# Transposing x on TensorE, pacing the modulation by matmuls issued, and loading early weights from GpSimd's queue

## The chip, the cores and the metric

One core of a Trainium2 chip runs the program. The metric is device time in microseconds of one execution; before the change its median is 1635.82 us over three runs. The engines are TensorE (PE, matmuls; PEld is its weight load), VectorE (DVE), ScalarE (ACT), GpSimd (POOL) and SyncE (SP, which here only issues DMAs). Each engine works through its own instructions in order.

## What is computed

A residual block on x of 512 x 2048: adaLN modulation, one wide projection, two branches (dilated attention and mLSTM), two output projections and a last norm. The early stage, which the change touches, is this part of the reference:

```python
mod = c @ w_ada[l] + b_ada[l]
shift, scale, gate = jnp.split(mod, 3, axis=-1)
h = rmsnorm(x, norm_gain[l]) * (1.0 + scale[:, None]) + shift[:, None]
proj = h @ w_in[l]
```

All is float32. Each product of float32 matrices is made of three matmuls on rounded parts: `a = hi + lo`, and hi\*hi, hi\*lo and lo\*hi are summed.

## The kernel before

h is held transposed: 16 tiles, k = 0 to 15, each of 128 features by 512 positions. The early stage makes these tiles one by one and multiplies each at once.

For one k these steps are needed, with their names in the code. (a) Modulation: four passes of DVE (L338, `modulation`), two halves of 1024 for scale and two for shift, each over a 512 KB tile `y` of `ada`, 64 in all. Call one pass a half. (b) A small product `gs` on DVE (L393), then ACT applies scale and shift to x (L396, `modulated`) and casts it to its rounded part, the tile `ha` or `hb` (L172, in `split`); the rest of that split, `lo`, is a subtraction (L173), which GpSimd makes for k > 0. (c) The stationary weights come as `ws[k]`, 128x768, in two parts of 384: ACT casts each to `hi`, DVE subtracts to `lo`. Then 18 matmuls of 512 columns (`first_products`, L280) add to six PSUM banks.

Ten more column blocks of the projection, the extras (`extra_products`), are not accumulated over all k in PSUM. They are done in five groups of k (`GROUPS`), so (g, n) is 6 matmuls for the short groups 0 and 4, and 12 for the long ones. The table `TURNS` tells after which k each pair of extras is issued. For group 0 ACT copies the PSUM bank to SBUF (L515), for later groups DVE adds it to what is there (L517). Their weights' `lo` parts are made by GpSimd. In all the stage has 288 matmuls of first products and 480 of extras.

Order: nothing is scheduled by a tool. Each engine's order is the order of the code. `prepare` issues the casts and subtractions of weights about three parts ahead of their matmuls, `hi` and `lo` have four buffers each, and `modulate(n)` issues halves until n are done. Before the change it is called so that the four halves of the next k are spread over the matmuls of this k (`next_pieces`). SP issues all loads from one list, `loads`: `y`, and weights into `raw` (three buffers) and `more` (one). x comes already transposed (`xT`), four of the 16 tiles ahead of the constants.

The norm's statistic (`first_norm`): ACT squares the 16 tiles, PE and DVE sum them over features, and the reciprocal root stands as 128x512, one value for each position in each partition. Each tile is multiplied by it (L388, `normed`), the first on DVE and the others on GpSimd, four k ahead.

After this stage come the V projection of the mLSTM (`vblock`, matmuls of 258 columns), and then all the rest of the program.

Of the kernel before, what the change touches and what calls it, by code (L numbers as in the profile page):

```python
# [104 lines left out]
def block_kernel(ctx: ExitStack, tc, xT, x, c, cst, abias, ada, ws, wu, wv, fgain, out):  # L105
# [72 lines left out]
    stream, loads, pieces, ready, late, tasks, beside = [], [], [], [], [], [], []  # L178
    at = {"load": 0, "split": 0, "half": 0, "piece": 0, "raw": 0, "more": 0, "y": 0}
# [9 lines left out]
    def add(u):  # L189
        stream.append(u)  # L190
        loads.append(u)

    def load_ahead():
        while at["load"] < len(loads):
            u = loads[at["load"]]
            if u.ring == "any":
                u.ring = "raw" if at["raw"] < RAW or "more" not in tags else "more"
            if at[u.ring] == {"raw": RAW, "more": MORE, "y": ADA}[u.ring]:
                if u.ring == "more":
                    u.ring = "any"  # L200
                break
            if u.at_load:
                u.at_load()
            u.raw = S(u.ring)
# [4 lines left out]
    def prepare():
# [9 lines left out]
        else:  # L219
# [75 lines left out]
    def load_x(n):  # L295
        for _ in range(n):
            t = S("gm")
            dma(t, xT[len(xt)])
            xt.append(t)
# [1228 lines left out]
```

## Time and profile before

| | us |
|---|---|
| median of three runs (1635.78 to 1636.86) | 1635.82 |
| the profiled execution | 1637.23 |
| its span, first to last instruction | 1635.4 |
| first matmul of the early stage's products starts | 36.07 |
| last one starts, and the V projection's first | 246.54, 246.77 |

The profile shows, for each engine, when an instruction ran and what ended the wait ahead of it. The granted clock is given as a share of 2.4 GHz, so 0.50 is the lower level of 1.2 GHz. A matmul's duration holds the pipeline's drain, so for matmuls in a row the distance between starts is what counts.

### The profile page before, as it was taken

The page shows a single profiled execution, that of the slowest core. Times are in us where ns is not written, and L with a number is a line of the kernel's source. Part 1 is how long each engine was busy: PE and PEld are TensorE (multiplying, and loading weights), DVE is VectorE, ACT ScalarE, POOL GpSimd, SP SyncE. Part 2 cuts the span into 40 slices and gives each one's busy share as a digit, 9 for nine tenths or more (in the row PEclk, how much of TensorE's full clock was granted, in tenths as well). Part 3 has the DMA queues.
Part 4 walks back from the last instruction along what each step waited for, and adds up shares of the span by engine and source line. Part 5 has one row for each costly group of instructions (what it writes and reads, how often), then busy time and mean ns, then how long its engine had stood idle before and what let it go on. Part 6 is the DMA issues. An engine that isn't in the chain of part 4 may idle for free.

```text
span 1635.4 us, 24961 instructions
## 1 busy us (share of the span) xinstructions
PE 1565.2 (96%) x9686; PEld 1388.3 (85%) x9686; DVE 1147.9 (70%) x1933; ACT 704.6 (43%) x1189; POOL 139.8 (9%) x112
## 2 busy tenths in 40 slices
PE   3799899999999999999999999999999999999997
PEld 1576689988888888999999999999999788878887
DVE  6788867667746568888788887888896444474445
ACT  3332344335525434455454454454443843343234
POOL 2665540000000000000000000000000000000000
PEclk7999999999999999999999999999999999999999
DMA  8677735665222344344443444444444654432333
GB/s 313 241 276 273 272 113 168 223 217 179 90 94 74 104 163 159 139 152 130 142 144 124 146 145 137 144 142 132 133 161 149 216 176 137 176 105 95 125 117 129
DMA packets 93879, 260.01 MB, mean 159 GB/s; under 512 B 10424, under 2 KB 14648, under 8 KB 93760
## 3 DMA queue, kind: packets, MB, share of 16 engines
q1 hardware_dynamic: 79928, 233.24, 41.6%
q10 hardware_dynamic: 13832, 25.18, 4.4%
q8 instruction: 76, 1.25, 0.3%
q14 instruction: 43, 0.35, 0.1%
HBM read 229.02 MB, written 29.36 MB: 158 GB/s over the span
## 4 chain that ended last, share of the span: by engine, by line
PE 71%; DVE 13%; issue 6%; ACT 4%; DMA 3%; POOL 1%; SPq 0%; ACTq 0%; DVEq 0%; POOLq 0%
PE ps L280 47%; PE ps L807 23%; DVE y L338 3%; DVE lo L173 2%; ACT sh L172 2%; DVE cs L780 1%; DVE e L822 1%; DVE cs L784 1%; DVE cs L785 1%; DMA raw<-ws 1%; DVE sl L173 1%; DVE al L786 1%; DMA p<-kept 1%; DMA more<-ws 1%; ACT gm L396 1%
## 5 line engine op out<-in xcount | busy, mean ns | idle before, releaser
L173 DVE TENSOR_TENSOR lo<-raw,hi 128x512 fp32r<-128x512 f32 (+2 forms) x238 | 177.5, 751 | 172.1 <-ACT hi L172 171.7
L172 ACT CAST hi<-raw 128x512 fp32r<-128x512 f32 (+3 forms) x276 | 161.2, 596 | 277.9 <-PE ps L280 227.4
L807 PE MATMUL ps<-t,sh 128*128 128x256 f32 x1344 | 245.3, 282 | 0.0
L807 PEld LDWEIGHTS ps<-t,sh 128*128 128x128 f32 x1344 | 208.0, 190 | 0.0
L807 PE MATMUL ps<-t,sl 128*128 128x256 f32 x672 | 189.3, 282 | 0.0
L779 ACT CAST ah<-raw 128x768 fp32r<-128x768 f32 x112 | 93.6, 836 | 204.8 <-issue 105.2
L280 PE MATMUL ps<-ha,hi 128*128 128x512 f32 x384 | 126.5, 409 | 26.1 <-ACT ha L172 17.2
L173 DVE TENSOR_TENSOR sl<-cs,sh 128x1024 fp32r<-128x1024 f32 x112 | 137.3, 1226 | 16.0 <-ACT sh L172 15.7
L172 ACT CAST sh<-cs 128x1024 fp32r<-128x1024 f32 x112 | 117.6, 1050 | 67.8 <-DVE cs L785 67.4
L786 DVE TENSOR_TENSOR al<-raw,ah 128x768 fp32r<-128x768 f32 x112 | 106.9, 955 | 52.8 <-ACT ah L779 52.6
L280 PE MATMUL ps<-hi,h 128*128 128x512 f32 (+1 forms) x512 | 143.6, 366 | 0.0
L280 PE MATMUL ps<-hi,ha 128*128 128x258 f32 (+1 forms) x512 | 129.8, 339 | 0.0
L280 PE MATMUL ps<-hi,hb 128*128 128x258 f32 (+1 forms) x512 | 129.3, 339 | 0.0
L807 PEld LDWEIGHTS ps<-t,sl 128*128 128x128 f32 x672 | 127.8, 190 | 0.0
L280 PE MATMUL ps<-hb,hi 128*128 128x512 f32 x384 | 122.0, 397 | 1.6 <-POOL hb L173 1.6
L280 PEld LDWEIGHTS ps<-ha,hi 128*128 128x128 f32 x384 | 73.9, 195 | 48.3 <-ACT ha L172 19.2
L280 PEld LDWEIGHTS ps<-hi,h 128*128 128x128 f32 x512 | 91.8, 188 | 17.0
L807 PE MATMUL ps<-hb,ah 128*128 128x256 f32 x448 | 87.1, 287 | 11.5 <-DVE e L822 9.9
L280 PEld LDWEIGHTS ps<-hi,ha 128*128 128x128 f32 x512 | 87.8, 188 | 11.4 <-issue 0.4
L280 PEld LDWEIGHTS ps<-hi,hb 128*128 128x128 f32 x512 | 87.9, 188 | 10.8
L280 PE MATMUL ps<-lo,h 128*128 128x512 f32 (+1 forms) x256 | 93.9, 367 | 2.4 <-DVE lo L173 2.4
L280 PE MATMUL ps<-h,hi 128*128 128x512 f32 x286 | 89.6, 395 | 0.0
(276 smaller groups left out, 3461.8 us busy)
## 6 DMA issues: line engine op xcount, KB each, us to landing
raw<-wu SPq DMA_DIRECT2D x223, 512.0 KB, 3.6
y<-ada SPq DMA_DIRECT2D x64, 512.0 KB, 7.3
g<-kept SPq DMA_DIRECT2D x56, 256.0 KB, 3.9
kept<-e ACTq DMA_DIRECT2D x56, 256.0 KB, 2.5
raw<-ada SPq DMA_DIRECT2D x24, 512.0 KB, 3.7
more<-wu SPq DMA_DIRECT2D x16, 512.0 KB, 3.5
raw<-wv SPq DMA_DIRECT2D x12, 516.0 KB, 3.7
kept<-g ACTq DMA_DIRECT2D x20, 256.0 KB, 4.2
```

Of the source, the lines that this page charges most:

```text
L172: nc.scalar.copy(hi, src)
L173: (low or nc.vector).tensor_tensor(lo, src, as32(hi), ALU.subtract)
L280: nc.tensor.matmul(ps, a, b, start=first and n == 0, stop=last and n == 2)
L338: nc.vector.tensor_tensor_reduce(out=raw[:, :1024], in0=raw[:, :1024], in1=cb[half][:, :1024], scale=1.0, scalar=bmod[:, col : col + 1] if ...
L396: nc.scalar.activation(xt[k], xt[k], AF.Identity, bias=mods[:, k : k + 1], scale=gs)
L779: nc.scalar.copy(ah, r[:, HT : 4 * HT])
L780: nc.vector.tensor_tensor(two(s[:, : 2 * HT]), two(r[:, HT : 3 * HT]), r[:, :HT].unsqueeze(1).to_broadcast([P, 2, HT]), ALU.add,)
L784: nc.vector.tensor_tensor(s[:, 2 * HT : 3 * HT], s[:, :HT], r[:, 2 * HT : 3 * HT], ALU.add)
L785: nc.vector.tensor_tensor(s[:, 3 * HT :], s[:, 2 * HT : 3 * HT], r[:, 3 * HT : 4 * HT], ALU.add)
L786: nc.vector.tensor_tensor(al, r[:, HT : 4 * HT], as32(ah), ALU.subtract)
L807: nc.tensor.matmul(banks[bank][:, n * HT : (n + 1) * HT], x[:, w], y, start=count[bank] == 1, stop=count[bank] == 24 * len(BANKS[bank]),)
L822: nc.vector.tensor_tensor(v[:, 0:2, :], twice(v[:, 4, :]), two(bb), ALU.add)
```

## The change

- x is loaded as it lies, 16 tiles of 128 positions by 512 features, tile j\*4+t. The squares are summed along the rows as they are made (ten on ACT, six on DVE), so the statistic is one column for each of four tiles. `normed(j)` scales the four tiles of 512 features (for j = 0 two on ACT and two on DVE, for j = 1 to 3 all on ACT), and `turned(k)` transposes on PE: four 128x128 transposes into one PSUM bank, which ACT copies to SBUF (for k = 0 modulation reads the bank itself). `turned(0..3)` stand ahead of the first products, then two after each of the first products k = 0 to 5; `normed(1)` stands in `first_norm`, `normed(2)` and `normed(3)` after the first products of k = 1 and k = 3.
- All subtractions that GpSimd made, of h and of the extras' weights, are made on DVE.
- `TURNS`: all ten extras of group 0 are issued after k = 1; none after k = 2, 3 and 4. From k = 5 the table is as before.
- Pacing: the number of halves issued follows the number of matmuls issued, 6 plus one for each ten, with the need of the next k as a floor.
- Loads: `loads` is two lists. `y` stays on SP's queue; weights into `raw` and `more` are issued from GpSimd's queue as long as the pool `heads` is open (through the V_A blocks), and need not stand behind `y`.

Line numbers of the kernel after are about 2 to 26 higher. The core of the diff:

```diff
 TURNS = {
-    1: [(0, 0)], 2: [(0, 2), (0, 4)], 3: [(0, 6)], 4: [(0, 8)],
+    1: [(0, 0), (0, 2), (0, 4), (0, 6), (0, 8)],
     5: [(1, 0), (1, 2)], 6: [(1, 4)], 7: [(1, 6)], 8: [(1, 8)],
...
-            dma(u.raw[:, : u.width], u.src)
...
+                (nc.gpsimd if "heads" in open_parts and u.ring != "y" else nc.sync).dma_start(u.raw[:, : u.width], u.src)
...
     def first_norm():
...
+        for j in range(NT):
+            for t in range(NT):
+                to, junk = sums[:, t, j : j + 1], S("hb")
+                if (j * NT + t) % 8 in (2, 5, 7):
+                    nc.vector.tensor_tensor_reduce(
...
+                else:
+                    nc.scalar.activation(junk, xn[j][t], AF.Square, accum_out=to)
...
+        nc.vector.tensor_reduce(rstd, sums, mybir.AxisListType.X, ALU.add)
+        nc.scalar.activation(rstd, rstd, AF.Sqrt, bias=eps, scale=1.0 / D)
         nc.vector.reciprocal(rstd, rstd)
-        rs.append(rstd)
-        normed(0, nc.vector)
+        normed(0, True)
+        for k in range(4):
+            turned(k)
         modulate(3)
         for _ in range(2):
             prepare()
         modulate(4)
-        for k in range(1, 4):
-            normed(k, nc.gpsimd)
+        normed(1)
...
+    def normed(j, both=False):
+
+        for t in range(NT):
+            r = rstd[:, t : t + 1]
+            if both and t % 2:
+                nc.vector.tensor_scalar(xn[j][t], xn[j][t], r, None, ALU.mult)
+            else:
+                nc.scalar.activation(xn[j][t], xn[j][t], AF.Copy, scale=r)
+
+    def turned(k):
+
+        ps = PS("m")
+        for t in range(NT):
+            nc.tensor.transpose(ps[:, t * P : (t + 1) * P], xn[k // 4][t][:, k % 4 * P : (k % 4 + 1) * P], ident)
+        if k == 0:
+            xt.append(ps)
+        else:
+            xt.append(S("hb" if k < HK else "gm"))
+            nc.scalar.copy(xt[k], ps)
...
-            split(xt[k], a, b, nc.gpsimd if k else None)
+            split(xt[k], a, b)
...
+    AHEAD, PACE = 2, 10
+    emitted = [0]
+
+    def next_pieces(n):
+
+        emitted[0] += n
+        modulate(4 + AHEAD + emitted[0] // PACE)
...
+            if half == 1 and k < 6:
+                for i in range(2 * k + 4, 2 * k + 6):
+                    turned(i)
+                if k % 2 == 1 and k < 4:
+                    normed(k // 2 + 2)
...
-                Unit(next(src)[:, :width], width, [extra_products(g, n), extra_products(g, n + 1)], low=nc.gpsimd)
...
+                Unit(next(src)[:, :width], width, [extra_products(g, n), extra_products(g, n + 1)])
```

How the order moves, at three places. On ACT, between the modulated tiles of k = 3 and k = 4, before (gm_101 is x of k = 4, raw_345 holds the weights of k = 3, more_391 those of two extras):

```order
L172 CAST hi_469<-raw_345 128x384
L515 COPY g_474<-ps_460 128x512
L172 CAST hi_485<-raw_345 128x384
L515 COPY g_489<-ps_476 128x512
L172 CAST hi_509<-more_391 128x256
L515 COPY g_513<-ps_491 128x512
L172 CAST hi_526<-more_391 128x256
L396 ACTIVATE gm_101<-gm_101,mods,gs_542 128x512
```

The same place after (hb_325 is x of k = 4, gm_661 and gm_668 those of k = 10 and 11, gm_117 to gm_123 the four tiles of `normed(3)`, raw_531 holds the weights of k = 5):

```order
L172 CAST hi_643<-raw_499 128x384
L409 COPY gm_661<-ps_656 128x512
L409 COPY gm_668<-ps_663 128x512
L398 ACTIVATE gm_117<-gm_117,rstd 128x512
L398 ACTIVATE gm_119<-gm_119,rstd 128x512
L398 ACTIVATE gm_121<-gm_121,rstd 128x512
L398 ACTIVATE gm_123<-gm_123,rstd 128x512
L172 CAST hi_680<-raw_531 128x384
L420 ACTIVATE hb_325<-hb_325,mods,gs_685 128x512
```

The copies of the extras are gone from here, and two copies of transposes and four scalings stand ahead of the cast hi_680.

On DVE, up to the last half for k = 6 and its `gs`, before:

```order
L173 TENSOR_TENSOR lo_644<-raw_498,hi_643 128x384
L338 ISA y_614,mods<-y_614,w_134,acc_641 128x1024
L338 ISA mods 128x1
L338 ISA y_616,acc_697<-y_616,w_133,bmod 128x1024
L338 ISA acc_697 128x1
L338 ISA y_618,mods<-y_618,w_134,acc_697 128x1024
L338 ISA mods 128x1
L393 TENSOR_TENSOR gs_717<-mods,cs 128x1
```

And after (ps_846 and ps_864 are the banks of the last two extras that are issued ahead of k = 6; ha_892 is its rounded tile):

```order
L542 TENSOR_TENSOR g_451<-g_451,ps_846 128x512
L340 ISA y_678,acc_879<-y_678,w_132,bmod 128x1024
L340 ISA acc_879 128x1
L173 TENSOR_TENSOR lo_884<-raw_738,hi_883 128x512
L542 TENSOR_TENSOR g_477<-g_477,ps_864 128x512
L340 ISA y_693,mods<-y_693,w_133,acc_879 128x1024
L340 ISA mods 128x1
L414 TENSOR_TENSOR gs_889<-mods,cs 128x1
L173 TENSOR_TENSOR ha_892<-hb_389,ha_892 128x512
```

The last half of k = 6 now stands behind the sum that reads the last extra's bank, and the subtraction for h has come to DVE, right behind `gs`.

On GpSimd, behind the broadcasts of c, before:

```order
L388 TENSOR_TENSOR gm_94<-gm_94,w_164 128x512
L388 TENSOR_TENSOR gm_96<-gm_96,w_164 128x512
L388 TENSOR_TENSOR gm_98<-gm_98,w_164 128x512
L388 TENSOR_TENSOR gm_101<-gm_101,w_164 128x512
L173 TENSOR_TENSOR ha_293<-gm_94,ha_293 128x512
L388 TENSOR_TENSOR gm_103<-gm_103,w_164 128x512
L173 TENSOR_TENSOR lo_318<-raw_159,hi_317 128x256
```

And after:

```order
L207 DMA raw_144<-ws 128x768
L207 DMA raw_156<-ws 128x768
L207 DMA raw_158<-wu 128x512
L207 DMA more_160<-wu 128x512
L207 DMA raw_252<-wu 128x512
L207 DMA raw_334<-wu 128x512
```

GpSimd's arithmetic is gone from the early stage, and the first four weight loads wait for no buffer.

## Rows read from the trace of the kernel before

**Rows 1.** the page's chain that ended last, share of the span by line

```profile
PE ps L280 47%; PE ps L807 23%; DVE y L338 3%; DVE lo L173 2%; ACT sh L172 2%; DVE cs L780 1%; DVE e L822 1%; DVE cs L784 1%; DVE cs L785 1%; DMA raw<-ws 1%; DVE sl L173 1%; DVE al L786 1%; DMA p<-kept 1%; DMA more<-ws 1%; ACT gm L396 1%
```

**Rows 2.** windows: us; busy us (xinstructions) by engine, TensorE's granted clock, DMA share, GB/s

```profile
0.00:36.07 36.07, 9.15 (x11) 2.31 (x11) 21.76 (x28) 14.49 (x24) 11.54 (x12) 0.74 0.88 328
36.07:100.00 63.93, 52.68 (x190) 38.83 (x191) 52.67 (x66) 21.98 (x45) 35.05 (x23) 0.91 0.69 248
100.00:200.00 100.00, 91.51 (x379) 70.11 (x378) 84.59 (x105) 28.49 (x51) 58.24 (x34) 1.00 0.75 269
200.00:246.77 46.77, 46.77 (x202) 37.79 (x201) 30.58 (x44) 24.22 (x45) 20.58 (x23) 1.00 0.42 143
246.77:1635.40 1388.63, 1365.06 (x8909) 1239.31 (x8907) 958.32 (x1693) 615.46 (x1027) 14.44 (x20) 1.00 0.42 143
```

**Rows 3.** groups by form, first 260 us: busy us, mean ns | idle us before, releasers

```profile
L280 PE MATMUL ps<-ha,hi 128*128 128x512 f32 x256 | 86.0, 415 | 26.1 <-ACT ha L172 17.2 <-ACT hi L172 4.5 <-ACT g L515 2.4
L280 PE MATMUL ps<-hb,hi 128*128 128x512 f32 x256 | 81.7, 398 | 1.6 <-POOL hb L173 1.6
L280 PE MATMUL ps<-ha,lo 128*128 128x512 f32 x128 | 52.9, 413 | 2.1 <-DVE lo L173 2.1
L280 PE MATMUL ps<-hb,lo 128*128 128x512 f32 x128 | 51.4, 401 | 6.3 <-DVE lo L173 6.3
```

**Rows 4.** timeline of PE, two places: start us, us, instruction

```profile
246.54 0.39 PE L280 MATMUL ps<-hb,lo 128*128 128x512 f32 x1
246.77 0.28 PE L280 MATMUL ps<-hi,ha 128*128 128x258 f32 x1
...
424.46 0.60 PE L982 MATMUL ps<-cs,w 128*128 128x128 f32 x4
424.81 0.48 PE L280 MATMUL ps<-hb,hi 128*128 128x512 f32 x1
```

**Rows 5.** timeline of DVE, k=8 to k=9: start us, us, [idle before]

```profile
124.46 0.16 DVE L393 TENSOR_TENSOR gs<-mods,cs 128x1 f32<-128x1 f32 x1
126.57 1.33 DVE L173 TENSOR_TENSOR lo<-raw,hi 128x384 fp32r<-128x384 f32 x1 [1.95 <-ACT hi L172]
127.83 2.31 DVE L338 CUSTOM_DVE_ANT_0 y<-y,w,bmod 128x1024 f32<-128x1024 f32 x1
...
131.60 0.67 DVE L517 TENSOR_TENSOR g<-g,ps 128x512 f32<-128x512 f32 x1
...
134.45 1.27 DVE L338 CUSTOM_DVE_ANT_0 y<-y,w,bmod 128x1024 f32<-128x1024 f32 x1
...
135.77 1.28 DVE L338 CUSTOM_DVE_ANT_0 y<-y,w,acc 128x1024 f32<-128x1024 f32 x1
...
136.98 0.15 DVE L393 TENSOR_TENSOR gs<-mods,cs 128x1 f32<-128x1 f32 x1
```

**Rows 6.** timeline of ACT at k=8

```profile
124.65 0.82 ACT L396 ACTIVATE gm<-gm,mods,gs 128x512 f32<-128x512 f32 x1 [8.13 <-DVE gs L393]
125.50 0.62 ACT L172 CAST hb<-gm 128x512 fp32r<-128x512 f32 x1
```

**Rows 7.** groups by form, ACT, whole span

```profile
L515 ACT COPY g<-ps 128x512 f32<-128x512 f32 x10 | 5.8, 582 | 0.9 <-PE ps L280 0.9
L1298 ACT ACTIVATE y<-y,fr 128x512 f32<-128x512 f32 x8 | 5.4, 716 | 0.9 <-DVE fr L1294 0.9
```

**Rows 8.** timeline of all engines, start of the program

```profile
8.54 8.03 ACT L366 ACTIVATE hb<-gm 128x512 f32<-128x512 f32 x12 [0.74 <-DMA gm<-xT]
...
24.00 8.36 POOL L388 TENSOR_TENSOR gm<-gm,w 128x512 f32<-128x512 f32 x4 [18.22 <-DVE w L374]
...
24.55 2.29 DVE L338 CUSTOM_DVE_ANT_0 y<-y,w,bmod 128x1024 f32<-128x1024 f32 x1
...
36.07 1.52 PE L280 MATMUL ps<-ha,hi 128*128 128x512 f32 x2 [16.27 <-ACT ha L172]
...
36.66 0.55 DVE L173 TENSOR_TENSOR lo<-raw,hi 128x384 fp32r<-128x384 f32 x1
```

More of the change, by code (lines that the diff above doesn't have):

```diff
@@ L104, in block_kernel @@
 @with_exitstack
[L105 removed]
+def block_kernel(ctx: ExitStack, tc, x, c, cst, abias, ada, ws, wu, wv, fgain, out):
     nc = tc.nc
@@ L177, in block_kernel @@
     pos = [0, 0]
-    stream, loads, pieces, ready, late, tasks, beside = [], [], [], [], [], [], []
-    at = {"load": 0, "split": 0, "half": 0, "piece": 0, "raw": 0, "more": 0, "y": 0}
+    stream, loads, pieces, ready, late, tasks, beside = [], {"y": [], "raw": []}, [], [], [], [], []
+    at = {"split": 0, "half": 0, "piece": 0, "raw": 0, "more": 0, "y": 0}
     def begin(*desc):
@@ L190, in add, with load_ahead @@
         stream.append(u)
[L191 to L204, printed above, removed]
-            dma(u.raw[:, : u.width], u.src)
-            at["load"] += 1
-            at[u.ring] += 1
+        loads["raw"].append(u)
+    def load_ahead(only=None, most=99):
+        for kind in [only] if only else loads:
+            while loads[kind] and most:
+                u = loads[kind][0]
+                if u.ring == "any":
+                    u.ring = "raw" if at["raw"] < RAW or "more" not in tags else "more"
+                if at[u.ring] == {"raw": RAW, "more": MORE, "y": ADA}[u.ring]:
+                    if u.ring == "more":
+                        u.ring = "any"
+                    break
+                if u.at_load:
+                    u.at_load()
+                u.raw = S(u.ring)
+                (nc.gpsimd if "heads" in open_parts and u.ring != "y" else nc.sync).dma_start(u.raw[:, : u.width], u.src)
+                loads[kind].pop(0)
+                at[u.ring] += 1
+                most -= 1
     def prepare():
@@ L293, in block_kernel, with load_x @@
     begin_part("heads", "left", y=(8, 1032), w=(4, 1024), gm=(17, 512), mk=(1, P))
[L295 to L299, printed above, removed]
+    xn = [[None] * NT for _ in range(NT)]
+    def load_x(j):
+        for t in range(NT):
+            xn[j][t] = S("gm")
+            dma(xn[j][t], x[t * P : (t + 1) * P, j * T : (j + 1) * T])
     crow = [S("g") for _ in range(4)]
@@ L308, in block_kernel @@
     tri = cs[:, C_TRI : C_TRI + P]
-    load_x(12)
+    for j in range(1, NT):
+        load_x(j)
     mask = S("mk")
@@ L380, in first_norm @@
         modulate(4)
-        for k in range(1, 4):
-            normed(k, nc.gpsimd)
-    rs = []
-    later = []
-    def normed(k, e):
-        e.tensor_tensor(xt[k], xt[k], rs[0], ALU.mult)
+        normed(1)
[8 more added lines that the diff above has]
+        ps = PS("m")
+        for t in range(NT):
+            nc.tensor.transpose(ps[:, t * P : (t + 1) * P], xn[k // 4][t][:, k % 4 * P : (k % 4 + 1) * P], ident)
[4 more added lines that the diff above has]
+            nc.scalar.copy(xt[k], ps)
     def modulated(k):
@@ L764, in pair_units @@
                 unit = Unit(src, ring="raw")
-                loads.append(unit)
+                loads["raw"].append(unit)
                 paired.append((d, u, unit))
```

53 lines of the change are left out of this document (19 added, 34 removed).

## The prediction, made before the run

> **What bounds the kernel now.** I read the summary of the chain first: TensorE's matmuls hold most of it, and DVE's modulation, weight subtractions and weight loads come in with a few per cent [rows 1]. The windows say where these few per cent lie. From 246.77 us to the end PE is busy for 98% at the full clock; before that it starts at 36.07 and is busy for 82% up to 100 us and for 92% from 100 to 200, and only from 200 without a gap [rows 2]. So only the stretch up to 246.77 can be won or lost, and what it ends later or earlier is passed on one to one.
>
> That stretch has 256+256+128+128 = 768 matmuls of 512 columns [rows 3], 0.232 us apart at the full clock [rows 4]: 178.2 us. From 36.1 to 246.8 are 210.7, so 32.5 are lost. The waits printed beside the four groups add up to 36.1, and without the first wait of 16.3 to 19.8 [rows 3, 8]. The other 12.7 are slow clock (0.91 up to 100 us [rows 2]) and restarts after waits.
>
> What PE waits for is a loop of DVE, 12.5 us for each k (124.46 to 136.98), while its 42 matmuls take 9.7. In it a half costs 2.31 us with GpSimd beside it and 1.32 and 1.21 without (starts 134.45, 135.77, 136.98), a 384-wide subtraction 1.33 against 0.55, and after `gs` DVE stands still for 1.95 until ACT has modulated, cast h and cast the weights [rows 5, 6, 8].
>
> **The change, part by part.** The sum is made against the profiled execution, 1637.23 us, which is 1.41 above the median of the runs; at the end I take that off.
>
> *Start.* ACT is through with the squares at 16.6, the first half starts at 24.55 and the first product at 36.07 [rows 8]. After: the statistic is four columns, so its matmuls and the 128x512 root and reciprocal go; the last square, a reduce, a root and a reciprocal on columns are some 0.9 us (an estimate from the small operations, 0.15 for `gs` [rows 5]), then two tiles of 0.72 on ACT beside two on DVE [rows 7], 1.4. Against it GpSimd's first four loads, 1.31 MB, no longer wait behind x and `y` on SP's queue and may take bandwidth from x: nothing at best, 1.31 MB at 328 GB/s = 4.0 us at worst [rows 2]; I take 1.3, since GpSimd has four broadcasts of c to make first, while x is loading. So the halves start at 16.6 + 0.9 + 1.4 + 1.3 = 20.2. Four halves at 1.27 are 5.1, two subtractions 1.0, and from `gs` to the first product 0.2 + 0.85 + 0.62 = 1.7 [rows 5, 6]: 28.0, a gain of 8.1 (from 5.4 to 9.4).
>
> *Transposes.* 64, of which 16 lie in the start. The other 48 are on PE's path: 4 take 0.35 [rows 4], so 4.2 us. Their copies cost ACT 0.48 each for its queue (0.58 less the overlap [rows 7]).
>
> *GpSimd's arithmetic.* Its end takes the halves from up to 2.31 to 1.27. On the other side DVE gets the subtractions for h and for the extras, 15 and 50, at 0.60 for 512 columns (the distance from 131.60 to the next [rows 5] is near that) and about 0.35 for 256. DVE's work for a k with two extras is then four halves 5.1, two subtractions of 0.5 and two of 0.6, two sums of 0.6, and 2.4 from `gs` to the end of h's subtraction: 10.9, where 12.5 stood. If that were all, the change would win.
>
> *What the new order adds.* The subtraction of h stands right behind `gs`, so DVE waits 1.7 for ACT there, no longer than now. But other waits are new, since ACT and DVE take their queues in order and these now hold things that wait for PE. I followed the queues from k = 0, with the prices above, 0.62 for a scaling and 0.5 for a cast:
> - k = 1: the cast of the first extra's weights stands behind two copies that wait for the transposes behind k = 0, and the last half of k = 1 behind its subtraction. Copies 1.0, cast 0.4, subtraction 0.3, half 1.2, `gs` to product 1.7: PE waits 4.6.
> - The ten extras behind k = 1: casts for the third stand behind the copies and the four scalings of `normed(2)` (2.5), and the sixth's bank is freed by a copy that stands behind the modulation of k = 2. Two extras run at once, 2.8, then PE waits 1.5 at the third and 1.7 at the sixth: 3.2.
> - k = 4: behind k = 3 the second copy 0.7, `normed(3)` 2.5, the cast hi_680 0.5, its subtraction 0.5, one half 1.25, `gs` to product 1.7: 7.2. With no extras behind k = 3 PE has nothing else.
> - k = 5, likewise: copy 0.6, cast 0.6, subtraction 0.6, two halves 2.5, 1.8: 6.1.
> - k = 6 and 7: the last half stands behind the sum that reads the last extra's bank: sum 0.65, half 1.25, 1.7: 3.6 each. k = 8 and 9 have one extra of 2.8 left to cover it: 2.1 and 0.8.
> - From k = 8 to 13 pacing asks for 4.2 halves in 42 matmuls: DVE 11.1 for PE's 9.7, so six times 1.4, 8.4; a lead of three parts, some 7 us, can take much of it. Between 0 and 8.4; I take 4.5.
>
> Together 35.7, where 19.8 stand now. Slow clock and restarts: 12.7 now; the new waits are longer but about a dozen, where twenty were; I take 10 (6 to 13).
>
> *The weights' queue.* No row shows a load from GpSimd's queue. Loads from SP's queue arrive in time: the groups of products print no wait for a DMA [rows 3], so there is nothing to gain either. With four buffers a load is issued three units ahead, over 10 us. So I take nothing, and as bounds nothing and 1 us for each of the 41 units. Here the Trainium skill speaks against the change: SBUF — State Buffer, in the box of the section on the two separate sides, says that GpSimd writes the descriptors of its DMAs itself and can't while DVE runs an operation in a 2-port mode. In this stage after the change that would be the two scalings of `normed(0)` on DVE and small ones, so by the rule too the sum gets nothing; no run here shows a load from that queue yet.
>
> *Sum.* 28.0 + 178.2 + 4.2 + 35.7 + 10 = 256.1 for the end of the stage, against 246.8: 9.3 later. 1637.2 + 9.3 = 1646.5, less 1.4: **1645 us**. With the bounds of the start (-1.3, +2.7), of the last wait (-4.5, +3.9) and of the clock (-4, +3) not all at one end, 1639 to 1653.
>
> **The rivals.**
> - *DVE's relief carries through* (faster). If ACT runs its casts early enough that the listed waits up to k = 9 shrink to nothing, 31.2 of the 35.7 go: 1614. If half of them go, 1629. It decides if the sum of 35.7 stays below 23, since 26.4 would make the stage end as before. For it: DVE has 1.6 us less work for each k, and the halves are issued up to one k ahead. Against: each listed wait is a chain of instructions in order on one queue, which no earlier start of another shortens. 0.20.
> - *No difference*: the start gains 8.1 and the waits grow by about that less the transposes, to between 23 and 30 instead of 35.7. 1632 to 1639. 0.14.
> - *Weights come late* (much slower). If a load from GpSimd's queue takes over 10 us from its buffer's release, each unit's cast waits. At 0.4 us for each of 41 units 16 more: 1661. The skill's rule above would do that if it held for all of DVE's operations. 0.12.
> - *The forecast*, 1645. 0.54.
>
> **How the numbers follow.** The forecast is the likeliest by itself. Leaving out about one in ten at either end, the range reaches down into the half-way case of the first rival, 1632, and up past the forecast's own end into the third, 1656. A measurement of this kernel tells about 0.2%, 3.3 us, from no change. Faster 0.20, within 0.2% 0.14, slower 0.54 + 0.12 = 0.66.
>
> **What would show it.** After, the first product starts near 28, halves take 1.27 with no long ones, and k = 4, 5, 6 and 7 each begin after a wait of PE of 3 to 8 us; ACT's casts before k = 4 and 5 stand behind copies and scalings, and the V projection starts near 256. A V projection that starts before 243, or waits at k = 4 and 5 under 3 us, would make the order of the queues a wrong reading; casts that wait for a DMA would mean the third rival. Past the V projection's start nothing should differ.

## The result, and the profile after

| | before | after |
|---|---|---|
| median, us | 1636.34 (4 runs, 1635.78 to 1637.29) | 1664.73 (4 runs, 1663.71 to 1665.32) |
| ratio, 95% interval | | 1.0172 [1.0155, 1.019] |
| profiled execution, its span | 1637.23, 1635.4 | 1665.32, 1663.4 |
| first product of the early stage | 36.07 | 31.75 |
| V projection's first matmul (stage end) | 246.77 | 270.24 |
| from there to the end of the span | 1388.6 | 1393.2 |

The change makes the kernel slower by 1.7%, 28 us. The forecast was 1645 (1632 to 1656): the direction held, the size did not. Of the 28.0 us between the spans 23.5 are in the early stage and 4.5 behind it.

Windows of after, cut at its own stage, as [rows 2] for before (stretch; length, then busy us by engine in the order PE, PEld, DVE, ACT, POOL; granted clock, DMA share, GB/s):

```profile
0.00:31.75 31.75, 3.95 (x17) 3.01 (x17) 11.88 (x31) 14.34 (x33) 6.00 (x13) 1.00 0.95 351
31.75:100.00 68.25, 48.34 (x191) 37.17 (x191) 38.16 (x72) 33.37 (x64) 5.35 (x10) 0.88 0.72 246
100.00:200.00 100.00, 89.34 (x341) 69.11 (x341) 66.53 (x116) 26.56 (x47) 8.02 (x15) 0.89 0.68 233
200.00:270.24 70.24, 67.69 (x288) 53.35 (x286) 51.65 (x92) 29.03 (x54) 8.01 (x15) 1.00 0.41 139
270.24:1663.40 1393.16, 1371.98 (x8909) 1246.14 (x8907) 959.07 (x1694) 615.55 (x1028) 60.70 (x113) 1.00 0.42 143
```

From 31.75 to 100 PE is busy for 71%, and its granted clock is 0.88 up to 100 and 0.89 up to 200, where before had 0.91 and 1.00 [rows 2]. DVE, which was the busy engine before, is busy for 56 to 67% only. So PE waits, and not for an engine that is full. The groups of products by form, as [rows 3] (busy us, mean ns | idle us before, releasers):

```profile
L281 PE MATMUL ps<-ha,hi 128*128 128x512 f32 x256 | 93.5, 447 | 32.8 <-ACT ha L172 29.4 <-ACT g L540 2.4 <-ACT hi L172 0.6
L281 PE MATMUL ps<-hb,hi 128*128 128x512 f32 x256 | 82.2, 402 | 5.1 <-ACT hb L172 2.9 <-DVE g L542 1.7 <-DVE hb L173 0.4
```

The many short waits of before, for DVE's `lo` and GpSimd's `ha`, are gone. In their place stand a few long ones for `ha`, the rounded part of h itself. Here they are on PE's timeline (start, us, instruction, the wait in brackets):

```profile
31.75 1.52 PE L281 MATMUL ps<-ha,hi 128*128 128x512 f32 x2 [5.00 <-ACT ha L172]
43.37 1.52 PE L281 MATMUL ps<-ha,hi 128*128 128x512 f32 x2 [4.26 <-ACT ha L172]
...
86.07 1.52 PE L281 MATMUL ps<-ha,hi 128*128 128x512 f32 x2 [6.94 <-ACT ha L172]
...
99.65 1.52 PE L281 MATMUL ps<-ha,hi 128*128 128x512 f32 x2 [6.07 <-ACT ha L172]
...
122.39 1.52 PE L281 MATMUL ps<-ha,hi 128*128 128x512 f32 x2 [3.55 <-ACT ha L172]
...
138.69 1.52 PE L281 MATMUL ps<-ha,hi 128*128 128x512 f32 x2 [3.55 <-ACT ha L172]
```

They are the first products of k = 0, 1, 4, 5, 6 and 7. The sum of the prediction can now be filled in: 31.75 + 178.2 (768 products) + 4.2 (transposes) + 33.1 (all idle time printed beside the product groups, less the first 5.0) + the rest = 270.24, so the rest, slow clock and restarts, is 23.0.

That rest can be placed. From the first product of a k to PE's next wait, take the time and subtract 0.232 us for each 512-wide matmul and 0.087 for each transpose: for k = 4 that is 26 instructions that took 7.51 us instead of 4.87, so 2.6 lost. In the same way 2.5 are lost behind the wait at k = 0, 3.4 at k = 1, 2.7 at k = 5, 3.0 at k = 6, 3.4 at k = 7 and 2.1 at k = 8: 19.7 of the 23.0. The windows around k = 4 show what it is:

```profile
80.00:82.00 2.00, 0.00 (x0) 0.00 (x0) 0.00 (x0) 2.00 (x4) 0.00 (x0) 1.00 0.92 236
82.00:84.00 2.00, 0.00 (x0) 0.00 (x0) 1.31 (x2) 0.66 (x2) 0.00 (x0) 0.92 0.52 213
84.00:86.00 2.00, 0.00 (x0) 0.00 (x0) 0.52 (x3) 1.41 (x3) 0.00 (x0) 0.50 0.23 39
86.00:88.00 2.00, 1.93 (x4) 1.30 (x5) 1.91 (x4) 0.43 (x2) 0.00 (x0) 0.50 0.90 315
88.00:90.00 2.00, 2.00 (x7) 1.52 (x6) 1.75 (x3) 0.00 (x0) 0.00 (x0) 0.50 0.61 166
90.00:92.00 2.00, 2.00 (x9) 1.63 (x8) 0.00 (x0) 0.00 (x0) 0.53 (x1) 0.87 0.85 287
```

PE stands still from 79 on; its clock falls from 1.00 to 0.50 (2.4 to 1.2 GHz) within the wait, and stays there for the first 4 to 5 us of work behind it. Windows behind the waits at k = 1, 5, 6, 7 and 8 show 0.50 too. At k = 0 the profile gives 1.00, though the products there lie 0.43 us apart as they do at k = 4; what slows them there isn't shown.

### The profile page after: what moved, and what is told of

The parts are those of the page before. It is cut to its first block, busy times and chain, and to the rows that moved or that the text cites. A ratio compares the mean times of both kernels' runs of the same rounds, so it can differ in the third digit from the quotient of the medians.

```text
span 1663.4 us, 25117 instructions
## 1 busy us (share of the span) xinstructions
PE 1581.3 (95%) x9740; PEld 1408.8 (85%) x9740; DVE 1127.3 (68%) x2001; ACT 718.9 (43%) x1222; POOL 88.1 (5%) x166
## 4 chain that ended last, share of the span: by engine, by line
PE 79%; DVE 9%; ACT 5%; issue 3%; DMA 3%; SPq 0%; ACTq 0%; DVEq 0%
PE ps L281 52%; PE ps L833 26%; DVE y L340 2%; DVE lo L173 1%; ACT sh L172 1%; DMA gm<-x 1%; DVE cs L806 1%; DVE e L848 1%; DMA p<-kept 1%; DMA g<-kept 1%; DVE sl L173 1%; DVE cs L810 0%; DVE cs L811 0%; PE ps L404 0%; DVE h L173 0%
## 5 line engine op out<-in xcount | busy, mean ns | idle before, releaser
L173 DVE TENSOR_TENSOR lo<-raw,hi 128x512 fp32r<-128x512 f32 (+3 forms) x276 | 181.0, 661 | 171.1 <-ACT hi L172 170.8
L833 PE MATMUL ps<-t,sh 128*128 128x256 f32 x1344 | 246.7, 283 | 0.0
L833 PEld LDWEIGHTS ps<-t,sh 128*128 128x128 f32 x1344 | 209.7, 192 | 0.0
L833 PE MATMUL ps<-t,sl 128*128 128x256 f32 x672 | 190.2, 283 | 0.0
L281 PE MATMUL ps<-ha,hi 128*128 128x512 f32 x384 | 134.0, 430 | 32.8 <-ACT ha L172 29.4
L833 PEld LDWEIGHTS ps<-t,sl 128*128 128x128 f32 x672 | 129.0, 192 | 0.0
L281 PEld LDWEIGHTS ps<-ha,hi 128*128 128x128 f32 x384 | 77.7, 206 | 57.2 <-ACT ha L172 31.3
L281 PEld LDWEIGHTS ps<-hi,ha 128*128 128x128 f32 x512 | 88.0, 188 | 11.5 <-issue 0.4
L833 PE MATMUL ps<-hb,ah 128*128 128x256 f32 x448 | 88.0, 289 | 7.6 <-DVE e L848 7.1
L281 PEld LDWEIGHTS ps<-hb,hi 128*128 128x128 f32 x384 | 72.2, 190 | 23.7 <-ACT hb L172 3.7
```

The costliest lines, as they stand in the source:

```text
L173: (low or nc.vector).tensor_tensor(lo, src, as32(hi), ALU.subtract)
L281: nc.tensor.matmul(ps, a, b, start=first and n == 0, stop=last and n == 2)
L833: nc.tensor.matmul(banks[bank][:, n * HT : (n + 1) * HT], x[:, w], y, start=count[bank] == 1, stop=count[bank] == 24 * len(BANKS[bank]),)
```

## Where each wait comes from

First k = 4. On ACT and DVE, from after's timeline:

```profile
78.74 1.07 ACT L409 COPY gm<-ps 128x512 f32<-128x512 f32 x2 [3.16 <-PE ps L404]
79.69 2.56 ACT L398 ACTIVATE gm<-gm,rstd 128x512 f32<-128x512 f32 x4
82.16 0.50 ACT L172 CAST hi<-raw 128x384 fp32r<-128x384 f32 x1
...
82.69 0.56 DVE L173 TENSOR_TENSOR lo<-raw,hi 128x384 fp32r<-128x384 f32 x1 [4.06 <-ACT hi L172]
83.16 1.28 DVE L340 CUSTOM_DVE_ANT_0 y<-y,w,acc 128x1024 f32<-128x1024 f32 x1
84.37 0.08 DVE L340 DVE_READ_ACCUMULATOR2_ANT mods<- 128x1 f32 x1
84.37 0.15 DVE L414 TENSOR_TENSOR gs<-mods,cs 128x1 f32<-128x1 f32 x1
```

The chain is the one that the prediction followed: copies, scalings, cast, subtraction, one half, `gs`. But the last half of k = 4, at 83.16, has nothing to do with what it waits behind. Its `y` is there, and DVE stood still for 4.06 us. It stands there because it was not issued earlier. The new pacing issues 6 halves plus one for each ten matmuls. At the start of k = 1 to 7 there have been 18, 96, 114, 132, 150, 216 and 258 matmuls, so the count allows 7, 15, 17, 19, 21, 27 and 31 halves; k needs 8, 12, 16, 20, 24, 28 and 32. At k = 1, and from k = 4 to 7, the last one or two come only by the floor, when the code has come to that k's own products. The old pacing had them all issued by then, and spread one by one over the parts of the k before. At k = 2 and 3 nothing is late in after: the 60 matmuls of the ten extras have pushed the count ahead. The experiments below tell this cause from the others that the prediction's list mixes with it: the grouping of the extras, ACT's copies and scalings, DVE's new subtractions and the weights' queue.

## Experiments

All ratios are to the kernel before, run on the same chip in the same set.

| run | first product | stage end | median, us | ratio, 95% interval |
|---|---|---|---|---|
| after | 31.75 | 270.24 | 1664.73 | 1.0172 [1.0155, 1.019] |
| e1 weights on SP's queue | 27.68 | 263.76 | 1660.66 | 1.015 [1.0135, 1.0165] |
| e2 old table | 31.66 | 279.58 | 1674.68 | 1.0235 [1.022, 1.025] |
| e3 subtractions on GpSimd | 31.07 | 287.09 | 1683.3 | 1.0288 [1.027, 1.0305] |
| e4 zero matmuls in the waits | 31.54 | 258.25 | 1653.25 | 1.0105 [1.009, 1.0121] |
| e5 old pacing | 31.59 | 236.82 | 1629.56 | 0.9956 [0.994, 0.9972] |
| e6 AHEAD = 6 | 31.39 | 240.75 | 1636.89 | 1.0006 [0.9996, 1.0016] |
| e7 x loaded transposed | 35.61 | 267.40 | 1657.16 | 1.0134 [1.0109, 1.0158] |
| e8 AHEAD = 6, h's subtraction later | 31.46 | 239.17 | 1635.04 | 0.9999 [0.9988, 1.0009] |
| e9 PACE = 8 | 30.98 | 253.94 | 1650.52 | 1.0095 [1.0079, 1.011] |
| e10 before with the new pacing | 35.32 | 297.14 | 1688.13 | 1.0325 [1.0309, 1.034] |
| e11 e5, first weights on SP's queue | 27.86 | 231.78 | 1628.4 | 0.996 [0.9945, 0.9975] |
| e12 e11 with zero matmuls | 28.59 | 232.46 | 1627.59 | 0.9958 [0.9942, 0.9975] |
| e13 e11 with AHEAD = 4 | 27.36 | 231.38 | 1627.8 | 0.9947 [0.9929, 0.9965] |
| e14 PACE = 8 with a cap | 31.13 | 251.51 | 1648.38 | 1.0075 [1.0059, 1.0091] |
| e15 e5, subtractions on GpSimd | 31.21 | 247.60 | 1642.77 | 1.004 [1.0024, 1.0056] |

### One part undone at a time

**The weights' queue.**

```diff
-                (nc.gpsimd if "heads" in open_parts and u.ring != "y" else nc.sync).dma_start(u.raw[:, : u.width], u.src)
+                nc.sync.dma_start(u.raw[:, : u.width], u.src)
```

> The kernel after, with the early stage's weight loads issued from SP's queue again (the two lists stay). Theory (order of ACT's and DVE's queues, and slow clock behind each long wait): only the start moves. x has the bandwidth for itself again, its last tile lands 3 to 4 us sooner, the first product starts at 28 to 29 instead of 31.75 and the V projection near 267 instead of 270.2; the waits of PE at k = 1, 4, 5, 6, 7 stay within 1 us of 4.3, 6.9, 6.1, 3.6, 3.6. Time near 1661. Rival (GpSimd's queue brings the weights late): most of these waits shrink too, and the time falls below 1650. Third: weights stuck behind y on one queue, casts that wait for a DMA, over 1668.

The first product came at 27.68 and the time was 4.1 us lower, as expected; the waits at k = 1, 4, 5, 6 and 7 stayed at 4.27, 6.94, 6.07, 3.55 and 3.55. So GpSimd's queue costs the start, and it is not what PE waits for behind it. The stage end came 6.5 us sooner, where some 3 were expected. The other 2.4 are time lost behind the same waits: 1.3 to 1.6 us less at k = 1, 7 and 8 (at k = 8 the granted clock stays at 1.00 this time, and 0.5 is lost instead of 2.1), 0.3 to 0.8 more at k = 0, 4, 5 and 6. One and the same wait doesn't always cost the same. DVE's wait for the tiles of x shows the start, in after first and then in e1:

```profile
16.98 0.69 DVE L371 CUSTOM_DVE_ANT_0 hb<-gm 128x512 f32<-128x512 f32 x1 [4.89 <-DMA gm<-x]
...
20.37 0.69 DVE L371 CUSTOM_DVE_ANT_0 hb<-gm 128x512 f32<-128x512 f32 x1 [0.64 <-DMA gm<-x]
```

```profile
16.40 0.69 DVE L371 CUSTOM_DVE_ANT_0 hb<-gm 128x512 f32<-128x512 f32 x1 [0.66 <-DMA gm<-x]
```

**The table.**

```diff
-    1: [(0, 0), (0, 2), (0, 4), (0, 6), (0, 8)],
+    1: [(0, 0)], 2: [(0, 2), (0, 4)], 3: [(0, 6)], 4: [(0, 8)],
```

> The kernel after, with the old table for group 0 (one pair of extras behind k = 1, two behind k = 2, one each behind k = 3 and 4). Theory: cover is only moved. The waits at k = 4 and 5 fall by the 2.8 us of a pair, to about 4.1 and 3.3, and new ones of 1 to 3 us come at k = 2 and 3, where after has none; each is shorter, so a part of the slow clock goes. Stage end 262 to 270, time 1657 to 1665. Rival (the grouping alone makes the loss): the waits at k = 4 and 5 go to nothing and no new ones come; with their slow clock that is 13.0 + 5.3 = 18 less, time near 1647.

Both were wrong: it is 9.3 us worse by the stage end. PE now waits 6.06 at k = 2 and 3.21 at k = 3, and still 6.06 and 4.68 at k = 4 and 5. Each pair that is moved leaves a hole and fills little of one: with the old table the count stands, by the same arithmetic, at 10, 15, 18 and 21 halves at the start of k = 2 to 5, where 12, 16, 20 and 24 are needed. The grouping, which the prediction blamed at k = 4 ("With no extras behind k = 3 PE has nothing else"), helps under the new pacing; no run has the old table with the old pacing.

**The subtractions.**

```diff
-            split(xt[k], a, b)
+            split(xt[k], a, b, nc.gpsimd if k else None)
...
-                Unit(next(src)[:, :width], width, [extra_products(g, n), extra_products(g, n + 1)])
+                Unit(next(src)[:, :width], width, [extra_products(g, n), extra_products(g, n + 1)], low=nc.gpsimd)
```

> The kernel after, with the subtractions of h (k > 0) and of the extras' weights on GpSimd again. Theory: DVE's amount of work does not set the waits, the order of the queues does; halves beside GpSimd cost up to 2.3 us again instead of 1.28, in exchange DVE is spared 1.1 us of subtractions for a k and its 1.6 us wait for ACT behind gs. The waits of PE at k = 4 to 7 stay or grow by 1 to 2 us each; time 1663 to 1680. Rival (DVE's added subtractions are the cause): the waits shrink by 1 to 3 us each and the time falls to 1645 to 1655.

18.6 us slower, somewhat more than expected. So taking the subtractions back from DVE is no cure under the new pacing; e15 below asks the same under the old. But GpSimd brings a cost of its own here, at k = 1:

```profile
39.76 0.42 ACT L172 CAST hi<-raw 128x256 fp32r<-128x256 f32 x1
...
48.68 0.71 POOL L173 TENSOR_TENSOR lo<-raw,hi 128x256 fp32r<-128x256 f32 x1 [10.37 <-issue]
...
50.67 0.79 PE L281 MATMUL ps<-ha,hi 128*128 128x512 f32 x1 [8.54 <-POOL ha L173]
```

GpSimd's first subtraction of weights, whose cast was done at 40.18, starts only at 48.68, when a row of six halves on DVE (40.00 to 47.74) is through; h's subtraction stands behind it, and PE waits 8.54 us. So the run doesn't show what the subtractions cost on DVE by themselves.

**x as it was.** `load_x`, `first_norm` and `normed` of before with `xT`, no `turned`; the rest of after stays.

> The kernel after, with x loaded transposed again and the statistic, the root and the scaling on GpSimd of before; table, pacing, weights' queue and subtractions on DVE as after. Theory: PE loses the 4.2 us of transposes, ACT the copies (1.0 of the wait at k = 1, 0.7 at k = 4, 0.6 at k = 5) and the scalings (2.5 at k = 4); the first product comes 4 to 6 us later, and GpSimd's scalings make some halves long again. Stage end 260 to 268, time 1655 to 1663. Rival (turning x on PE makes the loss): the waits at k = 4 and 5 go to nothing with their slow clock, 1640 to 1647.

7.6 us faster, as expected, and far from the rival. The waits at k = 4 and 5 fall to 3.64 and 2.96, those at k = 6 and 7 stay at 3.61. So copies and scalings on ACT lengthen two of the chains by some 3 us each, and PE saves the transposes. It isn't the main cause. (The profiled execution was the slowest of the four, 1662.58, so the stage end of 267.40 is on the high side.)

**The pacing.**

```diff
-    AHEAD, PACE = 2, 10
-    emitted = [0]
+    turn = []
+    AHEAD = 2
...
-        emitted[0] += n
-        modulate(4 + AHEAD + emitted[0] // PACE)
+        k, n, i = turn
+        modulate(4 * (k + 1) + AHEAD + 4 * (i + 1) // n)
+        turn[2] += 1
...
+                turn[:] = [k, 2 * (1 + len(TURNS.get(k, []))), 0]
```

> The kernel after, with the pacing of before (the four halves of the next k spread over the parts of this k). Theory: by matmuls issued, the count lags behind from k = 4 on, so that the last half of k = 6, 7, 8 and 9 comes only by the floor at its own turn, behind the sum that reads the last extra's bank. With the old pacing it stands two parts earlier: the waits of 3.55, 3.55, 2.10 and 0.77 fall under 1 each, and with their slow clock some 12 to 15 us go there. Against it the ten extras behind k = 1 carry 4 halves instead of 7 or 8, so k = 2 and 3 wait 2 to 4 us each. Stage end 258 to 266, time 1652 to 1660. Rival (the pacing does nothing, the waits at k = 6 to 9 are DVE's amount of work): time within 3 us of 1664.7 or above.

This is the cause. 35 us go, where 5 to 13 were expected, and the kernel is 0.4% faster than before. The expectation left the waits at k = 4 and 5 as they were; they fell as well, to 2.49 and 1.65. Under the old pacing the halves stand between subtractions, one at a time, as DVE's timeline of e5 shows ahead of k = 7:

```profile
108.21 1.28 DVE L340 CUSTOM_DVE_ANT_0 y<-y,w,bmod 128x1024 f32<-128x1024 f32 x1
109.42 0.08 DVE L340 DVE_READ_ACCUMULATOR2_ANT acc<- 128x1 f32 x1
109.42 0.69 DVE L173 TENSOR_TENSOR lo<-raw,hi 128x512 fp32r<-128x512 f32 x1
110.02 1.28 DVE L340 CUSTOM_DVE_ANT_0 y<-y,w,acc 128x1024 f32<-128x1024 f32 x1
```

### The pacing alone, in the kernel before

The same edit the other way round, in the kernel before.

> The kernel before, with nothing but the pacing of after (6 halves and one for each ten matmuls issued). Theory (the pacing alone makes the loss): the last two halves of nearly each k up to 8 are issued at its own turn, PE waits some 3 to 4 us at each in the place of 1 to 2.5, with slow clock behind it: 20 to 40 us more, time 1655 to 1676. Rival (the pacing costs only with the queues of after, with copies, scalings and subtractions in them): within 5 us of before.

53 us slower, beyond what was expected. From k = 6 to 9 PE's waits are those of after (3.58, 3.57, 2.10 and 0.77); k = 1 to 5 wait 2.5 to 3.3 each; and behind each stands GpSimd's subtraction, 0.9 to 1.8 more. PE's groups by form in the first 297 us:

```profile
L280 PE MATMUL ps<-ha,hi 128*128 128x512 f32 x256 | 94.5, 448 | 49.9 <-ACT ha L172 38.1 <-POOL ha L173 10.3 <-ACT hi L172 1.5
L280 PE MATMUL ps<-hb,hi 128*128 128x512 f32 x256 | 87.6, 423 | 11.7 <-DVE g L515 4.6 <-POOL hb L173 3.2 <-ACT hb L172 2.9
```

Not all of the 53 us are halves that are issued late. Near the end of the stage two halves wait over 8 us for `y` itself, which none does in after:

```profile
230.37 1.28 DVE L338 CUSTOM_DVE_ANT_0 y<-y,w,bmod 128x1024 f32<-128x1024 f32 x1 [8.58 <-DMA y<-ada]
...
247.02 1.28 DVE L338 CUSTOM_DVE_ANT_0 y<-y,w,bmod 128x1024 f32<-128x1024 f32 x1 [8.41 <-DMA y<-ada]
```

Behind them PE waits 1.63 us (232.19) and 4.63 us (251.17) for DVE. In this kernel `y` and the weights stand in one list; that this holds `y` up is argued, not shown.

With e5 this makes a square: the kernel before 1635 with the old pacing and 1688 with the new, the other parts of the change 1630 and 1665. The pacing costs 35 to 53 us; all the rest together gains 6 with the old pacing and 23 with the new.

### Is it lateness, or the spread?

**Everything a k earlier** (`AHEAD, PACE = 6, 10`), and the same with the subtraction of h put behind the next half.

> The kernel after, with AHEAD = 6 instead of 2: every half is issued one whole k earlier. Theory (the halves stand too late in DVE's queue): the waits at k = 4 to 9 go nearly all, with their slow clock, k = 1 loses 2 to 4 us of its wait; stage end 235 to 250, time 1630 to 1645. Rival 1 (y does not arrive earlier): DVE's halves wait for their DMA, time over 1655. Rival 2 (ACT's copies and scalings are what is late, whenever the halves run): the waits at k = 4 and 5 stay at 4 us or more and the time stays over 1650.

> As the run with AHEAD = 6, and the subtraction of h stands on DVE behind the next half instead of right behind gs, so DVE no longer stands still while ACT modulates and casts. Theory: where DVE is the bound (up to k = 5 or so) it gains up to 1.6 us for each k, 5 to 8 us over the run with AHEAD = 6; time 1625 to 1640. Rival (DVE was not the bound there): within 2 us of that run; or slower, since the second product of each k needs that subtraction, 1.3 us later.

e6 held: with lateness taken away 28 of the 35 us go. e8 is 1.9 us faster than e6, so its rival held: DVE's wait for ACT behind `gs` (1.53 us each time) is not what bounds.

**A faster count** (`PACE = 8`).

> The kernel after, with PACE = 8 instead of 10, one number. Theory (the count of matmuls lags: with 10 it stands at 15, 17, 19, 21, 27 halves at the start of k = 2 to 6, where 12, 16, 20, 24, 28 are needed, so from k = 3 on the last halves of a k are issued by the floor, at its own turn): with 8 it stands at 18, 20, 22, 24, 33, each k has its halves issued before its turn. The waits at k = 4 to 9 fall to 2 us or less each, stage end near 237 to 242, time 1629 to 1636, like the run with the old pacing. Rival (what the old pacing gained was its form, halves spread over the parts of a k): time over 1645.

The rival held. Only 14 us come back, though no k has too few halves at its turn. (k = 5 has just enough, 24, where the old pacing is two ahead, and still waits 3.57.) PE now waits for sums and weight subtractions, 4.84 us for a sum at 160.46. One reading was that the count runs too far ahead (by the same arithmetic 43 halves at the start of k = 8, where 36 are needed). So e14 caps it at the lead of the old pacing:

```diff
-        modulate(4 + AHEAD + emitted[0] // PACE)
+        modulate(min(4 + AHEAD + emitted[0] // PACE, 4 * (now[0] + 2) + AHEAD))
```

> The kernel after with PACE = 8 and a cap: never more halves than the old pacing has issued at the end of the same k. Theory (PACE = 8 lost by running too far ahead, its halves stand in DVE's queue ahead of sums and subtractions): the waits of 3.1 us in the ten extras and of 4.8 us near 160 go, stage end 236 to 242, time 1629 to 1636. Rival (it is the spread over the parts of a k that counts): the stage end stays above 250, time 1646 to 1652.

That reading falls: 1648.4. The wait of 4.84 is gone, that of 3.13 in the ten extras and one of 3.48 at k = 5 are there, and eight others have come, 1.31 to 1.34 us each, one for each k from 6 to 13. DVE and PE at one of them:

```profile
138.94 1.28 DVE L340 CUSTOM_DVE_ANT_0 y<-y,w,bmod 128x1024 f32<-128x1024 f32 x1
...
140.27 1.28 DVE L340 CUSTOM_DVE_ANT_0 y<-y,w,acc 128x1024 f32<-128x1024 f32 x1
...
141.48 0.69 DVE L173 TENSOR_TENSOR lo<-raw,hi 128x512 fp32r<-128x512 f32 x1
...
142.22 0.50 PE L281 MATMUL ps<-ha,lo 128*128 128x512 f32 x1 [1.32 <-DVE lo L173]
```

The cap opens at the turn of a k, and the halves that it held back are issued together. Two stand in front of a subtraction whose cast was done at 138.83 and that PE needs next; in e5 one half stands there. So both count: halves that are issued late stretch the chain to h, and halves that are issued in a bunch stretch the chain to the weights. The old pacing avoids both, since it divides the four halves over the parts of each k, whether that k has 18 matmuls or 78.

### The clock

```diff
+    FILL = {0: 14, 3: 26, 4: 22, 5: 12, 6: 12, 7: 6}
+    zero = S("w", F32R)[:, :P]
+    nc.vector.tensor_scalar(zero, cs[:, C_ID : C_ID + P], 0.0, None, ALU.mult)
...
+        for _ in range(FILL[k]):
+            nc.tensor.matmul(first[0], zero, hh[0], start=False, stop=False)
...
+            if half == 1 and k in FILL and k not in TURNS:
+                fill(k)
...
+            if g == 1 and n in (3, 5, 7):
+                fill({3: 5, 5: 6, 7: 7}[n])
```

> The kernel after, with extra matmuls of a zero matrix (they add nothing to the sums) where PE waits: 14 behind k = 0, 26 behind k = 3, 22 behind k = 4, 12 ahead of k = 6 and of k = 7, 6 ahead of k = 8, each fewer than fits in the wait at 0.232 us. Theory (the slow clock behind a long wait is a cost of its own): the granted clock stays at 1.00 over the waits, the 18 products of k = 1, 4, 5 and the first ones of 6, 7, 8 go 0.232 us apart instead of 0.43, and of the 2.1 to 3.4 us lost at each of these six restarts about 0.3 stays: 15 us in all, V projection near 255, time near 1650. Rival (the slow products come from something else, late weights or banks): the spacing stays, time 1662 to 1668.

11.5 us faster with 92 matmuls more. At k = 4, which now starts at 83.82, the clock stays up:

```profile
82.00:84.00 2.00, 0.99 (x5) 0.53 (x3) 0.47 (x4) 1.66 (x3) 0.00 (x0) 1.00 0.35 66
84.00:86.00 2.00, 1.77 (x7) 1.23 (x8) 1.96 (x4) 0.19 (x1) 0.00 (x0) 1.00 0.86 310
86.00:88.00 2.00, 2.00 (x10) 1.60 (x10) 1.50 (x3) 0.00 (x0) 0.20 (x1) 1.00 0.48 175
```

So about half of the 23.0 us of slow clock is shown to be a cost of its own, which goes when PE is kept at work in the wait.

### A better kernel, and what is left

> The run with the old pacing, and the weights that are loaded before the norm issued from SP's queue, behind x (the later ones stay on GpSimd's). Theory: as in the run with SP's queue, x lands 4 us sooner and the first product starts near 27.7; stage end 232 to 234, time 1624 to 1627. Rival (DVE bounds the halves of k = 1 to 5 by y's arrival, and y is not sooner): the first product moves, the stage end stays near 236.8, time over 1628.

> The run before this one, with zero matmuls in the waits that are left: 18 ahead of the first product, 8 behind k = 0, 6 behind k = 3, 4 behind k = 4. Theory: the slow clock behind these four waits, 2.1 to 3.0 us each in the run with the old pacing, goes for the most part: stage end 5 to 8 us sooner than without, time 1617 to 1621. Rival (the next wait grows by what is won, since DVE's halves set the time): within 2 us of the run without.

> The run with the old pacing and the early weights from SP's queue, with AHEAD = 4 instead of 2, so every half stands half a k earlier. Theory (what is left of the waits at k = 1, 4 and 5, 2.4, 2.5 and 1.6 us, is a half that comes too late): these waits shrink by 1 us or more each, stage end 225 to 230, time 1621 to 1627. Rival (more lead puts halves ahead of sums and subtractions that PE needs sooner, as with PACE = 8): new waits for sums, time 1630 to 1637, like the run with AHEAD = 6.

e11 starts 3.7 us sooner than e5 and its stage ends 5.0 sooner, in the profiles (e5's slowest execution, e11's fastest). The medians, 1628.4 and 1629.56, and the ratios, 0.996 and 0.9956, don't show it; runs of either kernel spread over 5 to 6 us, so it stays open whether the earlier start reaches the end. In e12 the zero matmuls ahead of the first product ran until 28.59, 0.7 us too long. k = 1, 4 and 5 start at 38.59, 75.92 and 84.86, against 37.95, 75.27 and 84.21 in e11, so what the clock gave went into longer waits for DVE's halves: the rival held. e13 traded its waits for `ha` against waits for copies and `lo`, and is no clear gain. e5, e11, e12 and e13 each beat both kernels, by 0.4 to 0.5% of before.

```diff
-            split(xt[k], a, b)
+            split(xt[k], a, b, nc.gpsimd if k else None)
```

The same edit as in e3, with the extras' weights, now under the old pacing:

> The kernel after with the old pacing, and with the subtractions of h (k > 0) and of the extras' weights on GpSimd again. Theory: GpSimd beside DVE makes halves up to 2.3 us long again; by the prediction's reckoning 12.5 us of DVE for a k instead of 10.9, 1.4 us over PE's 11.1 where it bounds, six to twelve times: 1638 to 1648. Rival (with the old pacing DVE has slack): within 3 us of 1629.6.

13 us slower than e5, as expected. Halves by form, in after first, then in e15:

```profile
L340 DVE CUSTOM_DVE_ANT_0 y<-y,w,acc 128x1024 f32<-128x1024 f32 x32 | 41.0, 1280 | 0.5
L340 DVE CUSTOM_DVE_ANT_0 y<-y,w,bmod 128x1024 f32<-128x1024 f32 x32 | 40.9, 1278 | 0.0
```

```profile
L340 DVE CUSTOM_DVE_ANT_0 y<-y,w,acc 128x1024 f32<-128x1024 f32 x32 | 65.1, 2033 | 0.8
L340 DVE CUSTOM_DVE_ANT_0 y<-y,w,bmod 128x1024 f32<-128x1024 f32 x32 | 45.1, 1408 | 0.0
```

Subtractions on GpSimd lengthen the 64 halves by 28 us. Taking GpSimd's subtractions off is the part of the change that gains. The other parts together (x turned on PE, the table, the queues) lose: e15 has them with the old pacing and is 6.6 us slower than before. Which of them loses it is open.

## The prediction, step by step

- **Start, 28.0.** Measured 31.75. The step that failed is the 1.3 us for GpSimd's first loads: they cost 4.1 (e1: 27.68 without them), just over its upper bound of 4.0. GpSimd issued them at 5.93 to 8.42, when only a part of x had landed, and they landed at 13.80 to 17.23. Without them the reckoning gives 26.7, 1.0 too early: in e1 the halves start at 18.86, as reckoned (18.9), and then DVE waits 1.02 for ACT's cast ahead of the two subtractions, which the sum left out.
- **Waits, 35.7.** Measured 33.1, and one by one: k = 1 4.6 and 4.26, the ten extras 3.2 and 2.64, k = 4 7.2 and 6.94, k = 5 6.1 and 6.07, k = 6 and 7 3.6 and 3.55, k = 8 2.1 and 2.32, k = 9 0.8 and 1.0. The last, DVE-bound k = 8 to 13, was 4.5 and is 2.3. Following the queues in order gave sizes to a few tenths. What it did not give is the cause. The list names for each wait what stands in front, and the prediction took the grouping of the extras and ACT's new work for the reason. It looked for the price of pacing only at k = 8 to 13, as too many halves; in truth the pacing issues too few at k = 1 and from k = 4 to 7, and undoing it removes most of the waits (e5), while undoing the grouping makes them worse (e2). Against its first rival it held that each wait is a chain in order on one queue, "which no earlier start of another shortens". That is the step that failed here: the last half was in these chains only because it was issued there, and issued earlier it is out of them (e5, e6).
- **Slow clock and restarts, 10 (6 to 13).** Measured 23.0. This is the step that failed in the sum, 13.0 of the 20 us by which the time was off. The prediction saw that the waits get longer and fewer and took that as a small gain. But before, the 12.7 us are restarts of 0.2 to 0.5 behind short waits and only three stretches of 1.6 to 2.8; after, each of seven waits of 2 to 7 us costs 2.1 to 3.4 behind it. e4 gives 11.5 us of it back. What one such wait costs is partly luck: e1, with the same waits, lost 2.4 us less behind them.
- **Transposes, 4.2; halves at 1.27; the weights' queue at nothing behind the start.** All held, to half a microsecond: a group of eight transposes takes 0.79 of PE's queue (73.04 to 73.83), so 4.7 for 48; 1.28 for a half; and no cast of the stage that waits for a DMA of weights. So the third rival, late weights, falls, and with it the rule in the Trainium skill's SBUF — State Buffer (the box of the section on the two separate sides) in the wide form in which that rival would need it. As the Trainium skill words it there, for operations in a 2-port mode alone, it isn't tested here: the two scalings of `normed(0)` ran at 22.02 to 22.90, and GpSimd issued no load between 8.42 and 29.19. The 41 loads from GpSimd's queue behind the start landed 2.8 to 7.6 us after their issue, 4.8 in the median, beside DVE's halves and subtractions; the median of `y` from SP's queue is 5.3.
- **DVE's relief carries through** (first rival). It does not in after, but in e5 it does, for 6 us, and e15 shows 13 us of relief, of which the other parts take back 7.
- **Past the V projection's start nothing should differ.** It does, by 4.5 us, and by 3.4 to 7.2 in every kernel built from after (1.6 in e10, built from before; one execution of each). The order of instructions there is the same on each engine, but for GpSimd's loads, and with these on SP's queue (e1) it is 4.9. One place shows on the timeline. Before, ACT loads a table and then waits for data; after, the load itself starts only when the data are there. ACT and PE, first in before, then in after:

```profile
1266.68 1.28 ACT L1158 ACT_TABLE_LOAD   x1
1273.08 0.63 ACT L1158 ACTIVATE g<-g 128x512 f32<-128x512 f32 x1 [5.12 <-DMA g<-kept]
...
1276.74 0.73 PE L280 MATMUL ps<-y,hi 128*128 128x512 f32 x2 [0.72 <-ACT hi L172]
```

```profile
1298.76 1.28 ACT L1184 ACT_TABLE_LOAD   x1 [6.62 <-DMA g<-kept]
...
1303.71 0.73 PE L281 MATMUL ps<-y,hi 128*128 128x512 f32 x2 [2.22 <-ACT hi L172]
```

That is 1.5 us and a slow restart, some 3.0 in all by the distance between the two timelines. Why the wait moved to the load is not settled. The other 1.6 us are spread: by the same distance after gains 1.8 us up to 805 us (before's time) and loses 3.5 from there to 1250, a little at each step of the products of L833, at a granted clock of 1.00. That is open too.

By its terms: 256.1 + 3.75 (start) + 13.0 (clock) - 2.6 (waits) = 270.25, the stage end measured, and 4.5 behind it. The range ended at 1656; the three upper bounds added up would have given 1655. The clock alone lies 10 us above its bound of 13. That the waits came to 33.1 for 35.7 is in part luck, since the last of them, 4.5, is 2.3.

## What to carry to other kernels

Work that feeds a later step should be issued by what that step needs and when, spread one by one over the steps before it. A count of something else that is only right on average (here matmuls, of which one k has 18 and another 78) issues it late in one place and in a bunch in another, and both cost. When a wait is found, ask what was issued too late before asking what stands in front of it. And price a long wait of TensorE with the restart behind it: here a few long waits cost more than many short ones, and what each cost varied from run to run.

## What the runs showed of the hardware

- In after, behind each of seven longer waits (2.1 to 6.9 us) the products ran slowly for a while, 2.1 to 3.4 us lost each time, at a granted clock of 0.50 behind six of them; the first windows behind the wait at k = 4 show it. In e1 the clock stayed at 1.00 over the same wait of 2.10 at k = 8, and 0.5 was lost. In e4 matmuls with a zero matrix in the wait at k = 4 kept it at 1.00.
- A half of DVE that takes 1.28 us alone took 2.03 and 1.41 in the mean when GpSimd had 65 subtractions to make in the same stage (e15). A subtraction of GpSimd's whose input was ready at 40.18 started at 48.68, behind a row of six halves on DVE that ended at 47.74 (e3).
- A table load on ACT can be held by the wait for the data of the instruction behind it: 1.28 us that then lie on the path instead of under the wait.
